# Eight-expert stage of a hybrid transformer: tokens gathered by indirect DMA from DRAM instead of by matmul, results parked in DRAM

## The chip, the cores and the metric

One NeuronCore of a Trainium2 chip runs the whole program. The metric is the device time of one execution in microseconds (us); the kernel before was timed in three runs, and one execution was profiled.

## The reference, cut to what matters

The program is two layers of a latent-diffusion trunk over 256 latent and 256 context tokens of width 1024, all in float32. The change touches the end of the second layer, where each of the 256 latent tokens goes to two of eight experts:

```python
def moe_swiglu(h, w_router, b_router, w_gate, w_up, w_down):
    logits = (h @ w_router + b_router).astype(jnp.float32)
    top_v, top_i = lax.top_k(logits, TOP_K)
    weights = jax.nn.softmax(top_v, axis=-1)
    combine = jnp.sum(jax.nn.one_hot(top_i, N_EXPERTS) * weights[..., None], axis=-2)
    y = jnp.zeros_like(h)
    for e in range(N_EXPERTS):
        y = y + combine[..., e:e + 1] * swiglu(h, w_gate[e], w_up[e], w_down[e])
    return y
```

Here h is the normalised and modulated token stream, `swiglu` is (silu(h Wg) * (h Wu)) Wd with 1024 -> 3584 -> 1024, and the result is scaled, added to the residual and normalised once more.

## The kernel before

**Precision.** Every large product is made of three fp32r matmuls (`mm3`, L212): high by high, high by low, low by high. So each weight tile of 128 x 2048 floats (a unit, 1 MB) is loaded from DRAM into a buffer `raw` by the SP queue (`load`, L156), copied to its rounded high part `wh` by ACT (L176), and its low part `wl` is subtracted by DVE (L177). There are three buffers of `wh` and `wl`, and eleven of `raw` in the expert stage.

**Experts.** For each expert up to 128 tokens are laid into 128 slots. The expert's hidden width is cut into seven chunks. A chunk takes two units of the gate weights, two of the up weights (`expert_in`, L1049, `half`, L1039), a transposition of the 128 x 512 result (`turn`, L1060: four PE transposes and a split into high and low), and two units of the down weights (`expert_out`, L1068), which is issued one chunk late. A unit is twelve matmuls of 512 columns, so a chunk is 72. Eight experts take 336 units.

**Tokens in.** `gather` (L1000) makes the slots' tokens by matmul: a 0/1 selection matrix `S` of 256 tokens by 128 slots (`slots`, L973) is multiplied with the tokens' high and low parts `hth`, `htl`, in eight groups of four matmuls of 128 columns, each group followed by one ACT and one DVE instruction which write `xg` (L1020, L1021). For experts 0 and 1 the tokens are not yet normalised, so that `S` carries the normaliser in two parts and a group has six matmuls. `normalize` (L986) then normalises `hth` and `htl` in place for the others.

**Results out.** When an expert's last chunk is done, its result stands in two PSUM tiles `ys`. `scatter_steps` (L1105) scales each, splits it into high and low, and multiplies it with the transposed `S` (`ST`, made by `slots_T`, L1080, with two PE transposes), two matmuls of 512 columns for each of two token tiles, and DVE adds the product, weighted by the token's share `cw`, to the residual `acc` (L1099). The last expert does this at once in plain float32 (`scatter_now`).

**Order.** `gather` and `normalize` are generators in a list `background`; `step` (L1031) advances the first by one yield behind every unit of gate or up weights. The framework then orders each engine's instructions itself: by program order, but one whose inputs it models as ready may be filled in ahead of an earlier one that it models as waiting. Weight loads are asked for eight units ahead, splits two units ahead.

Of the kernel before, what the change touches and what calls it, by code (L numbers as in the profile page):

```python
# [8 lines left out]
F32 = mybir.dt.float32  # L9
F32R = mybir.dt.float32r  # L10
# [6 lines left out]
P = 128  # L17
KD = 8
# [93 lines left out]
def _program(tc, A, out):  # L112
# [3 lines left out]
    def newpool(name, bufs, side="left"):  # L116
        return tc.alloc_tile_pool(name=name, bufs=bufs, side=side, reuse_waits="tile")
# [7 lines left out]
    pools = [const, rawp, whp, psp, smallp, xp]  # L125
# [13 lines left out]
    def ps_t():  # L139
        return psp.tile([P, 512], F32, tag="t", name=nm("pst"), bufs=2)  # L140
# [831 lines left out]

    def slots(p_, e, tag="S", by=None):  # L973
        if by is None:
            s_ = mop.tile([P, 2 * P], F32R, tag=tag, name=nm(tag), bufs=1)
        else:
            s_ = mop.tile([P, 512], F32R, tag=tag, name=nm(tag), bufs=1)[:, 0:2 * P]
        for tt in range(2):
            o, at = s_[:, tt * P:tt * P + P], p_[:, tt, e:e + 1]
            if by is None:  # L980
                vec.tensor_scalar(o, iota, at, None, ALU.is_equal)
            else:
                vec.tensor_scalar(o, iota, at, by[:, tt:tt + 1], ALU.is_equal, ALU.mult)
        return s_

    def normalize():  # L986
        for tt in range(2):
            for n in range(2):
                h, l = (t[:, tt, 512 * n:512 * n + 512] for t in (hth, htl))
                t, r = mop.tile([P, 512], F32, tag="yv", name=nm("t"), bufs=1), rs[:, tt:tt + 1]  # L990
                with tc.issue_after(first_gather[1].ins):
                    vec.tensor_scalar(t, l.bitcast(F32), r, None, ALU.mult)
                vec.scalar_tensor_tensor(t, h.bitcast(F32), r, t, ALU.mult, ALU.add)
                yield
                put_split(h, l, t)
                yield

    def gather(p_, e, raw=False):  # L1000
        S = []
        xg = mop1.tile([P, KD, 2, P], F32R, tag="xg", name=nm("xg"), bufs=2)

        def steps():
            if raw:
                s_ = slots(p_, e, "yh", rsh.bitcast(F32))
                terms = [(hth, s_), (htl, s_), (hth, slots(p_, e, "yl", rsl))]
            else:
                S.append(slots(p_, e))
                terms = [(hth, S[0]), (htl, S[0])]  # L1010
            yield
            for k in range(KD):
                pg = ps_mm() if front and k % 2 else ps_t()
                for i_, (hsrc, s_) in enumerate(terms):
                    for tt in range(2):
                        pe.matmul(pg[:, 0:P], lhsT=hsrc[:, tt, k * P:k * P + P], rhs=s_[:, tt * P:tt * P + P],
                                  start=(i_ == 0 and tt == 0), stop=(i_ == len(terms) - 1 and tt == 1))
                b = mod[:, 1, 24 + k, 0:1]
                hi, lo = xg[:, k, 0, :], xg[:, k, 1, :]
                ia = act.activation(hi, pg[:, 0:P], AF.Identity, bias=b)  # L1020
                iv = vec.scalar_tensor_tensor(lo, pg[:, 0:P], b, hi.bitcast(F32), ALU.add, ALU.subtract)  # L1021
                hold[:] = [ia, iv] if front else []
                yield
            if raw:
                S.append(slots(p_, e))
        return xg, S, steps()

    front = []
    background = []

    def step():  # L1031
# [3 lines left out]
    def drain(g):  # L1035
        for _ in g:
            pass
# [50 lines left out]
    def scaled(ys, n, tag="yv", bufs=1):  # L1088
        yv = mop.tile([P, 512], F32, tag=tag, name=nm(tag), bufs=bufs)
        vec.tensor_tensor(yv, ys[n], gf[:, 512 * n:512 * n + 512], ALU.mult)  # L1090
        return yv
# [10 lines left out]
        for n in range(2):  # L1102
            scatter(e, n, [(ST.bitcast(F32), scaled(ys, n, "a", 2))])

    def scatter_steps(e, ys, ST):  # L1105
        yv = scaled(ys, 0)
        for n in range(2):
            yh = mop.tile([P, 512], F32R, tag="yh", name=nm("yh"), bufs=1)
            yl = mop.tile([P, 512], F32R, tag="yl", name=nm("yl"), bufs=1)
            put_split(yh, yl, yv)  # L1110
            if n == 0:
                yv = scaled(ys, 1)
            yield
            scatter(e, n, [(ST, yh), (ST, yl)])

    prev = None
    xg, S, g = gather(pos, 0, True)
    front.append(0)
    drain(g)
    front.clear()  # L1120
    first_gather = list(hold)
    wp.release()
    xp.release()
# [12 lines left out]
    nxt, pend = (xg, S, g), []  # L1136

    def between():
        if prev is not None:
            turn(prev)  # L1140
        if pend:
            next(pend[0], None)

    def finish():
        expert_out(prev["e"], prev["c"], prev, prev["ys"])
        if prev["c"] == NCH - 1:
            pend[:] = [scatter_steps(prev["e"], prev["ys"], prev["ST"])]
            next(pend[0])
# [24 lines left out]
    between()  # L1173
    expert_out(prev["e"], prev["c"], prev, prev["ys"])
# [177 lines left out]
```

## Time and profile before

| | us |
|---|---|
| median of 3 runs (lowest to highest) | 1850.55 (1850.11 to 1851.01) |
| the profiled execution, its own time | 1851.12 |
| its span, first to last instruction | 1849.1 |

The expert stage fills the span from about 838 to 1837 us. Times in the rows further down are counted from the start of the span. PE is the matmul engine, PEld its weight loads, DVE the vector engine, ACT the scalar engine, POOL the GpSimd engine, SP the queue that issues the weight loads. A matmul's record lasts longer than its share of the engine, as successive matmuls overlap in the pipeline; the distance from start to start tells what one costs.

### The profile page before, as it was taken

Reading aid. Unit: us, or ns where it says so; the run is one execution under the profiler, and the core shown is the slowest. Engines: PE = TensorE matmul, PEld = TensorE weight load, DVE = VectorE, ACT = ScalarE, POOL = GpSimd, SP = SyncE. Lnnn points to the kernel's source line nnn. Section 1 sums busy time; section 2 is a strip of 40 time slices with the busy share of each in tenths; the row PEclk is TensorE's granted clock in tenths of the full one; section 3 lists DMA queues with packets and bytes.
Section 4 is the critical chain, followed back from the end, with each engine's and each line's share of the span. In section 5 each row is a group of like instructions: output and inputs, shape, how many; then the busy total and the mean of one; then the engine's idle time right before and its main releaser. Section 6 shows DMA issues by size and latency. Waiting matters only on the chain. (4 is left out here: it accounts for less than half of the span.)

```text
span 1849.1 us, 22123 instructions
## 1 busy us (share of the span) xinstructions
PE 1801.1 (97%) x8766; PEld 1438.1 (78%) x8766; DVE 1364.7 (74%) x1468; ACT 1039.8 (56%) x1082; POOL 0.2 (0%) x4
## 2 busy tenths in 40 slices
PE   6999998999999999999999999999999999999997
PEld 5775487888888878598888888888878888888885
DVE  5632645554455588658899899898898898988987
ACT  3323634222222245647677777777777777777774
POOL 0000000000000000000000000000000000000000
PEclk9999998999999999999999999999999999999999
DMA  9567321463344326039899999999999999999890
GB/s 364 186 234 267 122 96 57 151 225 137 114 160 168 114 54 199 22 137 358 329 354 370 326 370 356 348 350 362 352 339 356 351 351 352 367 351 347 331 416 35
DMA packets 68687, 475.03 MB, mean 257 GB/s; under 512 B 7520, under 2 KB 8160, under 8 KB 13024
## 3 DMA queue, kind: packets, MB, share of 16 engines
q1 hardware_dynamic: 66416, 469.27, 68.4%
q10 hardware_dynamic: 2160, 4.27, 0.7%
q8 instruction: 71, 1.16, 0.3%
q14 instruction: 40, 0.33, 0.1%
HBM read 470.36 MB, written 1.05 MB: 255 GB/s over the span
## 5 line engine op out<-in xcount | busy, mean ns | idle before, releaser
L177 DVE TENSOR_TENSOR wl<-raw,wh 128x2048 fp32r<-128x2048 f32 (+1 forms) x461 | 904.1, 1982 | 220.5 <-ACT wh L176 214.5
L176 ACT ACTIVATE wh<-raw 128x2048 fp32r<-128x2048 f32 (+1 forms) x461 | 763.3, 1670 | 415.9 <-PE mm L214 166.8
L213 PE MATMUL mm<-wh,xg 128*128 128x512 f32 x896 | 353.5, 395 | 0.0
L214 PE MATMUL mm<-wl,xg 128*128 128x512 f32 x896 | 352.3, 393 | 0.0
L215 PE MATMUL mm<-wh,xg 128*128 128x512 f32 x896 | 349.8, 390 | 0.0
L214 PEld LDWEIGHTS mm<-wl,xg 128*128 128x128 f32 x896 | 168.5, 188 | 35.1 <-DVE wl L177 1.8
L213 PE MATMUL mm<-hx,wh 128*128 128x512 f32 (+1 forms) x496 | 191.8, 391 | 3.8 <-ACT hx L400 3.8
L215 PEld LDWEIGHTS mm<-wh,xg 128*128 128x128 f32 x896 | 168.3, 188 | 34.2
L213 PEld LDWEIGHTS mm<-wh,xg 128*128 128x128 f32 x896 | 168.4, 188 | 33.6
L214 PE MATMUL mm<-hx,wh 128*128 128x512 f32 (+1 forms) x496 | 192.3, 388 | 0.0
L215 PE MATMUL mm<-hx,wl 128*128 128x512 f32 (+1 forms) x496 | 192.0, 387 | 0.0
L214 PE MATMUL pss<-wl,ahi 128*128 128x512 f32 x448 | 176.7, 395 | 1.3 <-DVE wl L177 1.3
L215 PE MATMUL pss<-wh,alo 128*128 128x512 f32 x448 | 174.4, 390 | 0.0
L213 PE MATMUL pss<-wh,ahi 128*128 128x512 f32 x448 | 168.2, 391 | 0.0
L213 PEld LDWEIGHTS mm<-hx,wh 128*128 128x128 f32 x496 | 94.3, 191 | 26.3 <-ACT hx L400 4.5
L214 PEld LDWEIGHTS mm<-hx,wh 128*128 128x128 f32 x496 | 94.4, 190 | 18.9
L215 PEld LDWEIGHTS mm<-hx,wl 128*128 128x128 f32 x496 | 94.1, 190 | 18.9
L214 PEld LDWEIGHTS pss<-wl,ahi 128*128 128x128 f32 x448 | 84.2, 188 | 20.3 <-DVE wl L177 3.9
L213 PEld LDWEIGHTS pss<-wh,ahi 128*128 128x128 f32 x448 | 84.2, 188 | 17.2
L215 PEld LDWEIGHTS pss<-wh,alo 128*128 128x128 f32 x448 | 84.2, 188 | 16.7
L409 DVE SCALAR_TENSOR_TENSOR x<-mm,mod,x 128x256 f32<-128x256 f32 x120 | 51.9, 478 | 38.8 <-PE mm L215 38.8
L215 PE MATMUL mm<-ah,wl 128*128 128x512 f32 x176 | 68.5, 389 | 0.0
(279 smaller groups left out, 1987.1 us busy)
## 6 DMA issues: line engine op xcount, KB each, us to landing
raw<-in_mg SPq DMA_DIRECT2D x112, 1024.0 KB, 7.1
raw<-in_mu SPq DMA_DIRECT2D x112, 1024.0 KB, 7.0
raw<-in_md SPq DMA_DIRECT2D x112, 1024.0 KB, 7.2
raw<-in_ada SPq DMA_DIRECT2D x48, 1024.0 KB, 5.3
raw<-in_na_in SPq DMA_DIRECT2D x10, 1024.0 KB, 5.8
raw<-in_fg SPq DMA_DIRECT2D x10, 1024.0 KB, 4.9
raw<-in_fu SPq DMA_DIRECT2D x10, 1024.0 KB, 4.9
raw<-in_fd SPq DMA_DIRECT2D x10, 1024.0 KB, 4.9
```

Of the source, the lines that this page charges most:

```text
L176: act.activation(h_, r_, AF.Copy)
L177: vec.tensor_tensor(l_, r_, h_.bitcast(F32), ALU.subtract)
L213: pe.matmul(ps, lhsT=lh, rhs=rh, start=start, stop=False)
L214: pe.matmul(ps, lhsT=lh, rhs=rl, start=False, stop=False)
L215: pe.matmul(ps, lhsT=ll, rhs=rh, start=False, stop=stop)
L409: vec.scalar_tensor_tensor(x[:, db, a:b], ps[:, a:b], mod[:, l, g0 + db, c:c + 1], x[:, db, a:b], ALU.mult, ALU.add)
```

## The change

A DRAM scratch `hrow` holds the 256 normalised tokens and `yrow` the results of seven experts. `normalize` now runs at the start of expert 0, adds the shift (transposed into rows, eight PE transposes), and stores four pieces of 256 KB to `hrow` through the POOL queue. `gather` for experts 1 to 7 computes the token number of each slot with two small matmuls of `S`, fetches 128 rows of 4 KB by an indirect DMA of the POOL queue into `xt`, and six yields later turns them with two groups of four PE transposes, each split by one ACT and one DVE instruction. For experts 0 to 6, `keep_rows` copies `ys` by ACT and stores two pieces of 256 KB to `yrow` through ACT's queue; there are no selection matmuls and no `ST` for them. At the start of expert 7, `fetch_rows` fetches each token's one or two rows by four indirect DMAs of 512 KB, and `combine` adds them, weighted, to `acc` in eight steps behind the units of the last two chunks. `row_numbers` computes the rows and weights with some twenty small DVE instructions. The first expert's gather is as it was. A gap tile grows from 56 to 72 words, which together with the new small tiles moves the fp32r operands behind it by a multiple of 256 bytes if each small tile takes a multiple of 32 bytes.

```diff
+    dramp = tc.alloc_tile_pool(name="dramp", bufs=1, space=bass.MemoryType.DRAM)
+    hrow = dramp.tile([TL, 1024], F32, tag="hrow", name="hrow")
+    yrow = dramp.tile([(NE - 1) * P, 1024], F32, tag="yrow", name="yrow")
...
-    mop.tile([P, 56], F32, tag="gap", name="gap2", bufs=1)
+    mop.tile([P, 72], F32, tag="gap", name="gap2", bufs=1)
...
     def normalize():
+        shift = []
+        for n in range(2):
+            pt = ps_t()
+            for j in range(4):
+                pe.transpose(pt[:, j * P:j * P + P], mod[:, 1, 24 + 4 * n + j, 0:1].to_broadcast([P, P]), ident)
+            shift.append(mop.tile([P, 512], F32, tag=("yh", "yl")[n], name=nm("shift"), bufs=1))
+            act.activation(shift[n], pt, AF.Copy)
+            yield
...
                 t, r = mop.tile([P, 512], F32, tag="yv", name=nm("t"), bufs=1), rs[:, tt:tt + 1]
                 with tc.issue_after(first_gather[1].ins):
-                    vec.tensor_scalar(t, l.bitcast(F32), r, None, ALU.mult)
+                    vec.scalar_tensor_tensor(t, l.bitcast(F32), r, shift[n], ALU.mult, ALU.add)
                 vec.scalar_tensor_tensor(t, h.bitcast(F32), r, t, ALU.mult, ALU.add)
+                nc.gpsimd.dma_start(hrow[tt * P:tt * P + P, 512 * n:512 * n + 512], t)
                 yield
-                put_split(h, l, t)
...
+    def gather(p_, e):
+        xg, S = new_xg(), []
+        def steps():
+            S.append(slots(p_, e))
+            yield
+            pi = ps_t()
+            for tt in range(2):
+                pe.matmul(pi[:, 0:2], lhsT=S[0][:, tt * P:tt * P + P].bitcast(F32), rhs=tokn[:, tt, :],
+                          start=(tt == 0), stop=(tt == 1))
+            idx = mop1.tile([P, 1], I32, tag="idx", name=nm("idx"), bufs=2)
+            vec.tensor_copy(idx, pi[:, 0:1])
+            xt = mop1.tile([P, 1024], F32, tag="htl", name=nm("xt"))
+            nc.gpsimd.indirect_dma_start(xt[:, :], None, hrow[:, :], bass.IndirectOffsetOnAxis(ap=idx[:, 0:1], axis=0))
+            for _ in range(6):
                 yield
+            for h in range(2):
+                pg = ps_t()
+                for j in range(4):
+                    pe.transpose(pg[:, j * P:j * P + P], xt[:, (4 * h + j) * P:(4 * h + j) * P + P], ident)
+                hi, lo = xg[:, 4 * h:4 * h + 4, 0, :], xg[:, 4 * h:4 * h + 4, 1, :]
+                put_split(hi, lo, pg.rearrange("p (k s) -> p k s", s=P))
                 yield
...
-    def scatter_steps(e, ys, ST):
+    def keep_rows(e, ys):
         for n in range(2):
+            yv = mop.tile([P, 512], F32, tag=("yh", "yl")[n], name=nm("yv"), bufs=1)
+            act.activation(yv, ys[n], AF.Copy)
+            nc.scalar.dma_start(yrow[e * P:e * P + P, 512 * n:512 * n + 512], yv)
...
+    def fetch_rows():
+        for tt in range(2):
+            yy = mop1.tile([P, 2, 1024], F32, tag=("hth", "xg")[tt], name=nm("yy"), bufs=1 + tt)
+            fetched.append(yy)
+            for i_ in range(2):
+                ri = mop1.tile([P, 1], I32, tag="nj", name=nm("nj"), bufs=4)
+                vec.tensor_copy(ri, rows[i_][0][:, tt:tt + 1])
+                nc.gpsimd.indirect_dma_start(yy[:, i_, :], None, yrow[:, :],
+                                             bass.IndirectOffsetOnAxis(ap=ri[:, 0:1], axis=0))
+    def combine():
+        for tt in range(2):
+            yy = fetched[tt]
+            for n in range(2):
+                h_ = slice(512 * n, 512 * n + 512)
+                a, b = yy[:, 0, h_], yy[:, 1, h_]
+                vec.tensor_scalar(a, a, rows[0][1][:, tt:tt + 1], None, ALU.mult)
+                vec.scalar_tensor_tensor(a, b, rows[1][1][:, tt:tt + 1], a, ALU.mult, ALU.add)
+                yield
+                vec.tensor_tensor(a, a, gf[:, h_], ALU.mult)
+                vec.tensor_tensor(acc[:, tt, h_], acc[:, tt, h_], a, ALU.add)
+                yield
...
             if c == 2:
-                ST = slots_T(S[0])
                 if e < NE - 1:
-                    nxt = gather(pos, e + 1, e == 0)
+                    nxt = gather(pos, e + 1)
                     background.append(nxt[2])
-                if e == 0:
-                    background.append(normalize())
+                else:
+                    ST = slots_T(S[0])
+                if e == 1:
+                    background.append(row_numbers())
+            if e == NE - 1 and c == 0:
+                fetch_rows()
+            if e == NE - 1 and c == 4:
+                background.append(combine())
```

## Rows read from the trace of the kernel before

**Rows 1.** The page's first part: busy time of each engine, its share of the span and its instructions.

```profile
PE 1801.1 (97%) x8766; PEld 1438.1 (78%) x8766; DVE 1364.7 (74%) x1468; ACT 1039.8 (56%) x1082; POOL 0.2 (0%) x4
```

**Rows 2.** Busy time by stretch: the expert stage, the part of it in which weights are loaded, and 40 us at the end of the loading. Columns: stretch, its length, then each engine's busy time and instructions, the granted PE clock, the DMA engines' busy share, GB/s.

```profile
838.00:1837.00 999.00, 992.75 (x4585) 818.03 (x4583) 886.52 (x599) 724.72 (x537) 0.00 (x0) 1.00 0.91 343
838.00:1806.00 968.00, 962.15 (x4455) 794.34 (x4454) 860.44 (x580) 707.38 (x521) 0.00 (x0) 1.00 0.94 354
1760.00:1800.00 40.00, 40.00 (x182) 33.09 (x181) 35.42 (x20) 29.48 (x20) 0.00 (x0) 1.00 1.01 419
```

**Rows 3.** Groups of instructions by line in the expert stage (838 to 1837 us): line, engine, operation, tiles, shapes, count, then busy time and mean ns of one, and the idle time before them.

```profile
L177 DVE TENSOR_TENSOR wl<-raw,wh 128x2048 fp32r<-128x2048 f32 x335 | 759.0, 2282 | 86.0 <-ACT wh L176 80.2 <-DMA raw<-in_md 3.7 <-DMA raw<-in_mg 1.1
L176 ACT ACTIVATE wh<-raw 128x2048 fp32r<-128x2048 f32 x335 | 639.8, 1913 | 165.0 <-PE mm L215 88.3 <-PE pss L215 64.2 <-DMA raw<-in_md 5.6
...
L1099 DVE SCALAR_TENSOR_TENSOR acc<-mm,cw,acc 128x512 f32<-128x512 f32 x32 | 23.2, 745 | 8.3 <-PE mm L1097 7.8
...
L1016 PE MATMUL pst<-S,hth 128*128 128x128 f32 x96 | 17.0, 248 | 1.0 <-DVE xg L1021 1.0
...
L1097 PE MATMUL mm<-yh,ST 128*128 128x512 f32 x28 | 11.2, 418 | 0.0
...
L218 ACT ACTIVATE yh<-yv 128x512 fp32r<-128x512 f32 x14 | 8.8, 626 | 1.4 <-DVE yv L1090 1.3
...
L1083 PE MATMUL pst<-c_ident,S 128*128 128x128 f32 x16 | 3.0, 271 | 0.0
L993 DVE SCALAR_TENSOR_TENSOR t<-hth,rs_y,t 128x512 f32<-128x512 f32 x4 | 3.0, 751 | 0.1
...
L1016 PE MATMUL pst<-yh,hth 128*128 128x128 f32 x16 | 2.9, 261 | 0.8 <-DVE xg L1021 0.8
...
L992 DVE TENSOR_SCALAR t<-htl,rs_y 128x512 f32<-128x512 f32 x4 | 1.9, 480 | 0.0
```

**Rows 4.** The round of one unit, in order of time (start, duration, engine, line, operation): PE ends a unit, ACT splits the unit three further on, DVE subtracts its low part (the row covers two units in a row), and PE first uses that low part. Between the two PE rows stand two whole units, with nothing but these matmuls: 26 steps from start to start.

```profile
1341.44 0.39 PE L215 MATMUL mm<-wh,xg 128*128 128x512 f32 x1
...
1341.87 1.92 ACT L176 ACTIVATE wh<-raw 128x2048 fp32r<-128x2048 f32 x1 [0.30 <-PE mm L215]
...
1341.60 4.52 DVE L177 TENSOR_TENSOR wl<-raw,wh 128x2048 fp32r<-128x2048 f32 x2 [0.80 <-ACT wh L176]
...
1347.34 0.39 PE L214 MATMUL pss<-wl,ahi 128*128 128x512 f32 x1
```

**Rows 5.** PE in order of time around one gather group of four matmuls (L1016): the matmul ahead of it, the group's first two, and the second matmul behind it.

```profile
1301.47 0.39 PE L215 MATMUL mm<-wh,xg 128*128 128x512 f32 x1
1301.70 0.33 PE L1016 MATMUL pst<-S,hth 128*128 128x128 f32 x2
...
1302.38 0.40 PE L214 MATMUL mm<-wl,xg 128*128 128x512 f32 x1
```

**Rows 6.** The same around a gather group of six (expert 1): the matmul ahead of it and the second one behind it.

```profile
896.92 0.39 PE L215 MATMUL mm<-wh,xg 128*128 128x512 f32 x1
...
898.04 0.40 PE L214 MATMUL pss<-wl,ahi 128*128 128x512 f32 x1
```

**Rows 7.** The same around a pair of scatter matmuls (L1097): the matmul ahead of it and the first one behind it.

```profile
1477.82 0.39 PE L213 MATMUL mm<-wh,xg 128*128 128x512 f32 x1
...
1478.50 0.39 PE L214 MATMUL mm<-wl,xg 128*128 128x512 f32 x1
```

**Rows 8.** The same around the two transposes of `ST` (L1083): the matmul ahead of them and the second one behind them.

```profile
1260.18 0.39 PE L215 MATMUL pss<-wh,alo 128*128 128x512 f32 x1
...
1260.86 0.39 PE L214 MATMUL mm<-wl,xg 128*128 128x512 f32 x1
```

**Rows 9.** The same around the four transposes of `turn` (L1063): the matmul ahead of them and the second one behind them.

```profile
1304.65 0.39 PE L215 MATMUL mm<-wh,xg 128*128 128x512 f32 x1
...
1305.55 0.40 PE L214 MATMUL mm<-wl,xg 128*128 128x512 f32 x1
```

**Rows 10.** Every wait of PE in the expert stage: who waited for whom, us in total, times, longest us.

```profile
PE pst L1063 <- DVE xg L1021: 2.8, 4, 0.7
PE pst L1016 <- DVE xg L1021: 1.8, 5, 0.6
PE pss L214 <- DVE wl L177: 1.3, 4, 0.7
```

**Rows 11.** The waits of SP's queue in the expert stage, in the same columns.

```profile
SPq L161 <- DVE wl L177: 647.0, 258, 8.5
...
SPq L161 <- DMA fg<-in_fg_row: 10.1, 2, 9.9
```

**Rows 12.** The last two weight loads as SP issues them, and the last unit as ACT splits it (in two halves).

```profile
1796.64 2.53 SPq L161 DMA_DIRECT2D raw<-in_md  x2
...
1825.96 2.00 ACT L176 ACTIVATE wh<-raw 128x1024 fp32r<-128x1024 f32 x2
```

**Rows 13.** DMA issues: target and source, queue, count, KB each, median us from issue to landing; and one issue of 256 KB as ACT's queue makes it.

```profile
raw<-in_mg SPq DMA_DIRECT2D x112, 1024.0 KB, 7.1
...
mkT<-krot SPq DMA_DIRECT2D x1, 2048.0 KB, 14.7
...
fg<-in_fg_row ACTq DMA_DIRECT2D x2, 256.0 KB, 2.9
...
1749.26 0.33 ACTq L1164 DMA_DIRECT2D fg<-in_fg_row  x1
```

More of the change, by code (lines that the diff above doesn't have):

```diff
@@ new lines, in new_xg, with first_gather_steps @@
+    def new_xg():
+        return mop1.tile([P, KD, 2, P], F32R, tag="xg", name=nm("xg"), bufs=2)
+    def first_gather_steps(xg):
+        s_ = slots(pos, 0, "yh", rsh.bitcast(F32))
+        terms = [(hth, s_), (htl, s_), (hth, slots(pos, 0, "yl", rsl))]
+        for k in range(KD):
+            pg = ps_mm() if k % 2 else ps_t()
+            for i_, (hsrc, s_) in enumerate(terms):
+                for tt in range(2):
+                    pe.matmul(pg[:, 0:P], lhsT=hsrc[:, tt, k * P:k * P + P], rhs=s_[:, tt * P:tt * P + P],
+                              start=(i_ == 0 and tt == 0), stop=(i_ == len(terms) - 1 and tt == 1))
+            b = mod[:, 1, 24 + k, 0:1]
+            hi, lo = xg[:, k, 0, :], xg[:, k, 1, :]
+            ia = act.activation(hi, pg[:, 0:P], AF.Identity, bias=b)
+            iv = vec.scalar_tensor_tensor(lo, pg[:, 0:P], b, hi.bitcast(F32), ALU.add, ALU.subtract)
+            hold[:] = [ia, iv]
@@ new lines, in row_numbers @@
+    def row_numbers():
+        sm = lambda t, w=8: mop1.tile([P, 2, w] if w > 1 else [P, 2], F32, tag=t, name=nm(t))
+        last = NE - 1
+        val, wv, eq = sm("nv"), sm("nw"), sm("ne")
+        vec.tensor_scalar(wv, pos, float(P) + 0.5, None, ALU.is_lt)
+        vec.tensor_tensor(wv, wv, msk, ALU.mult)
+        vec.memset(wv[:, :, last:last + 1], 0.0)
+        vec.tensor_tensor(val, pos, base.unsqueeze(1).to_broadcast([P, 2, 8]), ALU.add)
+        vec.tensor_tensor(val, val, wv, ALU.mult)
+        vec.tensor_tensor(wv, wv, cw, ALU.mult)
+        yield
+        for i_ in range(2):
+            row = sm(f"nr{i_}", 1)
+            vec.tensor_reduce(row, val, AX.X, ALU.max)
+            vec.tensor_tensor(eq, val, row.unsqueeze(2).to_broadcast([P, 2, 8]), ALU.is_equal)
+            t = sm("nt")
+            vec.tensor_tensor(t, eq, wv, ALU.mult)
+            w = sm(f"nc{i_}", 1)
+            vec.tensor_reduce(w, t, AX.X, ALU.add)
+            if i_ == 0:
+                vec.tensor_tensor(wv, wv, t, ALU.subtract)
+                vec.tensor_tensor(eq, eq, val, ALU.mult)
+                vec.tensor_tensor(val, val, eq, ALU.subtract)
+            vec.tensor_scalar(row, row, -1.0, 0.0, ALU.add, ALU.max)
+            ri = mop1.tile([P, 2], I32, tag=f"ni{i_}", name=nm("ni"))
+            vec.tensor_copy(ri, row)
+            rows.append((ri, w))
+            yield
@@ new lines, in _program @@
+    rows = []
+    def fetch_rows():
+        for tt in range(2):
+            yy = mop1.tile([P, 2, 1024], F32, tag=("hth", "xg")[tt], name=nm("yy"), bufs=1 + tt)
+            fetched.append(yy)
+            for i_ in range(2):
+                ri = mop1.tile([P, 1], I32, tag="nj", name=nm("nj"), bufs=4)
+                vec.tensor_copy(ri, rows[i_][0][:, tt:tt + 1])
+                nc.gpsimd.indirect_dma_start(yy[:, i_, :], None, yrow[:, :],
+                                             bass.IndirectOffsetOnAxis(ap=ri[:, 0:1], axis=0))
@@ new lines, in _program @@
+    fetched = []
+    def combine():
+        for tt in range(2):
+            yy = fetched[tt]
[7 more added lines that the diff above has]
+                vec.tensor_tensor(acc[:, tt, h_], acc[:, tt, h_], a, ALU.add)
+                yield
@@ L1116, in _program @@
     prev = None
[L1117 to L1120, printed above, removed]
+    xg = new_xg()
+    first_gather_steps(xg)
     first_gather = list(hold)
@@ L1135, in _program @@
     vec.tensor_tensor(cw, cw, ws.unsqueeze(2).to_broadcast([P, 2, 8]), ALU.mult)
-    nxt, pend = (xg, S, g), []
+    nxt = (xg, [], iter(()))
+    tokn = mop1.tile([P, 2, 2], F32, tag="tokn", name="tokn")
+    row0 = mop.tile([P, P], F32, tag="S", name="row0", bufs=1)
+    vec.tensor_tensor(row0, ident, iota, ALU.mult)
+    vec.tensor_reduce(tokn[:, 0, 0:1], row0, AX.X, ALU.add)
+    vec.tensor_scalar(tokn[:, 1, :], tokn[:, 0, 0:1].to_broadcast([P, 2]), float(P - 1), None, ALU.add)
+    vec.tensor_scalar(tokn[:, 0, :], tokn[:, 1, :], -float(P), None, ALU.add)
+    base = mop1.tile([P, 8], F32, tag="base", name="base")
+    vec.tensor_scalar(base, iota[:, 0:8], -1.0, float(P), ALU.add, ALU.mult)
+    background.append(normalize())
     def between():
@@ L1140, in between @@
             turn(prev)
-        if pend:
-            next(pend[0], None)
     def finish():
@@ L1146, in finish @@
         if prev["c"] == NCH - 1:
-            pend[:] = [scatter_steps(prev["e"], prev["ys"], prev["ST"])]
-            next(pend[0])
+            keep_rows(prev["e"], prev["ys"])
     ST = fg = None
```

34 lines of the change are left out of this document (1 added, 33 removed).

## The prediction, made before the changed kernel was run

> **What bounds the kernel now.** I read the page's busy shares first, then the expert stage by stretch, then PE's rows in order of time, and last who waits for whom. PE is busy 97% of the span [rows 1] and 992.8 of 999.0 us in the expert stage [rows 2]. A busy PE need not be a full one, so the distance from start to start decides: from 1341.44 to 1347.34 us there are 26 steps in 5.90 us, 0.227 us each [rows 4]. The stage has 336 units of 12 matmuls, 4032 x 0.227 = 915 us. Of 999 us, 84 are something else on PE: transposes, gather, scatter, and waits. That is the ground on which this change works, if nothing else is close to being the bound.
>
> Two things are close. First the round of a unit [rows 4]: PE ends unit j-3 (last start 1341.44 plus 0.39), ACT splits unit j until 1343.79, DVE has the low part at 1346.12, PE needs it at 1347.34. So 1.2 us are spare, and ACT or DVE work put into a round in one piece beyond 1.2 us stalls PE. Second the transport: 354 GB/s while weights are loaded, the DMA engines 94% busy [rows 2]. But SP waits 647 us for DVE to free a `raw` buffer [rows 11], so a load is issued when there is room, not when the DMA is free; the last loads are issued at 1796.6 to 1799.2 us and the last split begins at 1825.96, some 27 us later, where landing takes 7.1 [rows 12, 13]; and for 40 us the same transport ran at 419 GB/s [rows 2]. PE is the bound.
>
> **What leaves PE.** An insertion's cost is the distance around it less the ordinary steps in it.
> - Gather of experts 2 to 7: 96 `S,hth` rows at two a group are 48 groups [rows 3]. 1301.47 to 1302.38 is 0.91, less two steps 0.454: 0.456 us [rows 5]. 48 x 0.456 = 21.9.
> - Gather of expert 1: 16 / 2 = 8 groups of six [rows 3], 898.04 - 896.92 - 0.454 = 0.67 [rows 6]: 5.3.
> - Scatter of seven experts: 28 pairs [rows 3], 0.68 - 0.227 = 0.453 [rows 7]: 12.7.
> - `ST` of seven experts, 7 of the 8 pairs in L1083's 16 [rows 3], 0.68 - 0.454 = 0.226 [rows 8]: 1.6.
> - PE's waits, all at gather, scatter or just behind: 5.9 us in 13 [rows 10]. A wait is counted from the end of the record before, 0.39 long, while the next would have started after 0.227, so 13 x 0.163 = 2.1 more: 8.0.
>
> Together 49.5 us.
>
> **What comes onto PE.** A group of four transposes costs 0.90 - 0.454 = 0.446 [rows 9]. Seven gathers with two groups each: 6.2. Their two index matmuls: no such row; below the `ST` pair's 0.226 there is no row of two instructions, above it stands a gather group's 0.456 [rows 5]; I take 0.226 (same stationary width, hardly any columns), 1.6. `normalize`'s eight transposes: 0.9. Together 8.7, so PE's own work falls by 40.8 us.
>
> **What may make PE wait.** These are bounded, not read.
> - `normalize` has one buffer `t`; each of its three later pieces waits until the store has read it, and DVE waits with it, the next `wl` behind. A piece is two instructions of 0.75 [rows 3]; a store of 256 KB is nearest to the load of that size, 2.9 us under full load, at most a whole weight load's 7.1 [rows 13]. Within three units of 2.72: 3 x (1.5 + 2.9 - 2.72) - 1.2 = 3.8, or with 7.1 16. Below, nothing: the order on DVE is filled by readiness, and the same buffer cost DVE 0.1 us before [rows 3]. I take 3.
> - `keep_rows` puts two ACT copies of about 0.63 and two issues of 0.33 [rows 3, 13] between splits: 1.9 where `yh` and `ST` took 1.6 spread wider. 0 to 7 x (1.9 - 1.2) = 5; I take 2.
> - `combine` is sixteen DVE instructions on 512 columns, 4 x (0.48 + 3 x 0.75) = 10.9 us by the rows of that width [rows 3]. DVE idles 999.0 - 886.5 = 112 us in the stage, 14 per expert [rows 2], which holds it: 0. Kept at its written places, the four gate and up units of a chunk ask DVE for 4 x 2.28, half of `combine` (5.5) and the chunk's own two instructions of that width (1.5), 16.1, where PE takes 4 x 2.72 + 0.45 = 11.3. The deficit of 4.8 meets the spare 1.2 in the first chunk and the 2 x (2.72 - 2.28) = 0.9 that the down units give back in the second: 3.6 + 3.9 = 7.5. I take 2.
> - The small instructions of `row_numbers` and the new constants need only what the router leaves; they fall into DVE's gaps: 0 to 2, I take 1. The new gather's first steps may wait as the old one's did, 0.36 + 0.16 each: 0 to 3.6, I take 1.
> - The gathered rows: from the fetch to the first transposes lie six yields, 96 matmuls with the down weights between, 21.8 us, and a turn: 22.2. POOL issues nothing in this trace; 512 KB lie between 2.9 for 256 KB and 14.7 for 2 MB [rows 13]. All are covered: 0. `yrow` needs longer (four fetches, at worst 59 us) and has four chunks of 72 steps and a turn, 67 us.
> - The transport: 10.5 MB more (1 stored and 3.7 gathered of `hrow`, 3.7 stored and 2.1 fetched of `yrow`). From 838 to 1806 us 968 x 354 = 343 MB came [rows 2]; in a stage 32 us shorter that asks for 353.5 MB in 936 us, 378 GB/s, against the 419 seen: 0.
>
> Together 9 us, between 0 and 34.
>
> The row of the transport shows 419 GB/s for 40 us, at a PE clock as before [rows 2]. The Trainium skill ("DMA: Bandwidth & Descriptors", "Where 436 GB/s comes from") says that loads from HBM are bound at about 358 GB/s per core. By the row the sum stands; by that rule the added bytes and the shorter stage could not be had and the time would come out near rival 3's. The trace does not agree with the rule over those 40 us.
>
> **The sum.** The profiled execution took 1851.1 us; 1851.1 - 40.8 + 9 = 1819.3. The median of the runs is 0.6 below that execution: 1819 us. By the bounds of the waits, 1810 to 1844; its own range is 1809 to 1835.
>
> **Rivals.**
> 1. *Fetched rows come late.* PE stands at the transposes with everything behind it queued. If a fetch, with the index and the descriptors made on POOL, takes X us, each of seven experts loses X - 22.2. At 26 us that gives 1819 + 7 x 3.8 = 1846; with X = 24 to 28, 1832 to 1860. Against it stands a cover over twice any row of that size.
> 2. *POOL holds DVE* (slower). Writing and reading descriptors for 4 stores, 7 gathers and 4 fetches, POOL may lock DVE out for h us each, and `wl` is late by it. PE loses 15 x (h - 1.2). Above h = 3.3 this eats the whole 31 us; at 4 us it gives 1819 + 42 = 1861. Only the small spare of 1.2 us speaks for it; no row shows POOL at work beside DVE. The Trainium skill ("SBUF — State Buffer", "Who interferes with whom") says that a DVE instruction with two SBUF inputs, as L177 is, and a GpSimd instruction that reads SBUF block each other, the later one for the whole of the earlier; by it a fetch may start one `wl` late, or a `wl` one fetch late. No run here shows it yet.
> 3. *The transport is the bound* (no gain, or slower). Were 354 GB/s the ceiling, 353.5 MB would take 999 us and loading end at 1837; the last split 27 us after a load is then down to 7 of landing, so the tail behind the loads, 1849.1 - 1799.2 = 50, is 30, and the time 1867. It decides below 378. SP's waits and the 419 GB/s speak against it. For it: SP once stood 9.9 us behind a DMA that ACT issued [rows 11], and the change has ACT issue 14. If each of seven pairs costs SP that, the rest must run at 353.5 / (936 - 69) = 408 GB/s, just under the 419.
> 4. *The offset of the fp32r operands matters and is not kept.* What a step then costs no row shows; if 0.227 became 0.234 on all 4032, it is 28 us and the gain is gone: 1847. Against it: the sizes add up to a whole multiple of 256 bytes if they are rounded to 32.
>
> **How the numbers follow.** Forecast 0.70 (1809 to 1835); the same with the waits at their upper ends 0.08 (1835 to 1844); late rows 0.08; POOL on DVE 0.05; transport 0.05; offset 0.04. Above 1844 lie most of the last four, about 0.17, and 0.03 lie below 1808 if still more of PE's odd steps go. So the range is 1808 to 1844. A measurement of this kernel tells about 0.2%, 3.7 us, from no change. Slower: 0.04 of POOL, 0.03 of transport and 0.01 of late rows, 0.08; same, 0.04: half of the offset's and a little of each other rival; faster, the rest, 0.88.
>
> **What would show it.** In the changed profile: no L1097 in experts 0 to 6; PE's start-to-start still 0.227; the stage some 32 us shorter, an expert near 967 / 8 = 121 us in place of 125; PE's waits near 9 us, most of them in expert 0's first two chunks (behind `t`) and in expert 7; loading near 375 GB/s with SP still waiting for DVE. Wrong would be: PE waits at the transposes of `xt` (rival 1), `wl` longer than 2.28 us while POOL works (2), ACT's or DVE's splits waiting for `raw` (3), steps above 0.227 (4).

## The result, and the profile of the changed kernel

The changed kernel took 1840.4 us (median; 1839.0 to 1840.6) against 1850.8 before: ratio 0.9942, 95% interval 0.9926 to 0.9957. The forecast was 1819. The time lies inside the range (1808 to 1844), but only 10.4 us of the expected 31.5 came. The comparison is of fast runs; a fourth run of the kernel before, of 6385 us, is not one of them. Below, the expert stage counts from the first start of its matmuls to the last: 994.0 us before, 983.0 in the changed kernel.

Busy time by stretch, columns as in [rows 2]: the stage, the part of it in which weights are loaded, four microseconds of expert 0 (the third figure from the end is the granted PE clock), and the begin of expert 7 in slices of 5 us.

```profile
838.00:1827.00 989.00, 968.75 (x4369) 792.74 (x4368) 854.30 (x516) 712.19 (x488) 17.98 (x15) 0.99 0.90 357
838.00:1796.00 958.00, 938.94 (x4242) 769.71 (x4242) 828.22 (x496) 694.85 (x470) 17.98 (x15) 0.99 0.93 368
866.00:870.00 4.00, 4.00 (x12) 3.09 (x12) 4.00 (x5) 0.43 (x1) 0.14 (x1) 0.57 0.80 284
1695.00:1700.00 5.00, 5.00 (x26) 4.14 (x25) 4.00 (x3) 2.29 (x4) 0.00 (x0) 1.00 0.09 35
1700.00:1705.00 5.00, 3.69 (x17) 2.74 (x16) 3.35 (x2) 3.45 (x3) 0.00 (x0) 1.00 0.66 193
1705.00:1710.00 5.00, 4.08 (x18) 2.85 (x16) 1.23 (x1) 0.00 (x0) 0.00 (x0) 1.00 1.00 406
1710.00:1715.00 5.00, 0.82 (x2) 0.45 (x3) 2.29 (x1) 4.55 (x4) 3.53 (x3) 0.77 1.01 412
1715.00:1720.00 5.00, 4.98 (x12) 3.55 (x12) 0.01 (x1) 1.66 (x2) 1.44 (x2) 0.55 1.01 415
1720.00:1725.00 5.00, 2.27 (x6) 1.77 (x7) 4.77 (x5) 1.69 (x1) 0.00 (x0) 0.80 1.02 420
```

Where [rows 2] had PE idle for 6 of 999 us, it now idles for 20 of 989, although less is asked of it. In the first 30 us of expert 7 the transport first starves (35 GB/s), then runs at its best rate, PE does 12 instructions in a slice that holds 22 at full speed, and the granted clock falls to 0.55.

The waits of PE and of SP in the stage (838 to 1827), as in [rows 10, 11], and DVE's wait for the fetched rows. (`mm` are the gate and up products, `pss` the down products.)

```profile
PE mm L217 <- DVE wl L180: 10.8, 10, 1.8
PE pss L217 <- DVE wl L180: 4.9, 2, 2.8
PE mm L216 <- ACT wh L179: 3.3, 1, 3.3
...
SPq L164 <- DVE wl L180: 682.8, 278, 8.7
SPq L164 <- DMA yrow<-yv: 119.2, 14, 15.5
SPq L164 <- DMA fg<-in_fg_row: 10.5, 2, 5.3
...
DVE yy L1184 <- DMA yy<-yrow,nj: 5.3, 1, 5.3
```

PE's waits for `xg` in [rows 10] are gone; in their place it waits, 19 us in 13 pieces, for splits. SP stood behind the fourteen stores of `yrow` for 119 us. To see where it costs time, the stage's 336 units are cut into eight runs of 42, an expert's number, in the order in which PE does them. Each run counts from its first matmul to the next run's first, the last one to the first matmul of the stage's last unit; every run but the first begins two units into its expert (us, experts 0 to 7):

| kernel | e0 | e1 | e2 | e3 | e4 | e5 | e6 | e7 |
|---|---|---|---|---|---|---|---|---|
| before | 125.5 | 124.9 | 124.8 | 124.8 | 124.9 | 124.4 | 124.4 | 117.8 |
| changed | 124.4 | 119.2 | 121.1 | 121.0 | 121.3 | 121.0 | 120.7 | 131.8 |

Experts 1 to 6 gained 3.4 to 5.7 us each, expert 0 1.1, and expert 7 lost 14.

**A boundary between two experts** (1 to 2), in order of time: `keep_rows`' first copy and its issue, the split that they hold up, `wl` behind it, the second copy and issue, and PE.

```profile
1091.86 0.60 ACT L221 ACTIVATE ahi<-pst 128x512 fp32r<-128x512 f32 x1 [1.69 <-PE pst L1087]
1093.02 0.60 ACT L1132 ACTIVATE yv<-pss 128x512 f32<-128x512 f32 x1 [0.56 <-PE pss L218]
1093.65 0.33 ACTq L1133 DMA_DIRECT2D yrow<-yv  x1
1094.08 1.92 ACT L179 ACTIVATE wh<-raw 128x2048 fp32r<-128x2048 f32 x1 [0.46 <-DVE alo L222]
1095.90 0.58 ACT L1132 ACTIVATE yv<-pss 128x512 f32<-128x512 f32 x1
1096.02 2.29 DVE L180 TENSOR_TENSOR wl<-raw,wh 128x2048 fp32r<-128x2048 f32 x1 [2.08 <-ACT wh L179]
1096.50 0.33 ACTq L1133 DMA_DIRECT2D yrow<-yv  x1
1098.37 0.50 PE L217 MATMUL mm<-wl,xg 128*128 128x512 f32 x1 [1.28 <-DVE wl L180]
```

ACT is free at 1092.46, but the copy stands ahead of the split in its order and has to wait for PE's last matmul of that half; with the issue the split starts 1.62 us late, more than the spare 1.2 us. PE loses 1.45 us here, and 1.47 to 1.74 at each of the five boundaries that follow.

**The begin of expert 7**: SP's issues, then ACT, DVE, POOL and PE in order of time.

```profile
1684.88 16.24 SPq L164 DMA_DIRECT2D raw<-in_mg  x2
1701.22 6.06 SPq L164 DMA_DIRECT2D raw<-in_mu  x2
...
1698.71 0.33 ACTq L1133 DMA_DIRECT2D yrow<-yv  x1
...
1701.57 0.33 ACTq L1133 DMA_DIRECT2D yrow<-yv  x1
...
1710.45 1.91 ACT L179 ACTIVATE wh<-raw 128x2048 fp32r<-128x2048 f32 x1 [6.55 <-DMA raw<-in_mu]
1710.86 0.94 POOL L1173 DMA_INDIRECT yy<-yrow,nj  x1 [110.11 <-DMA yrow<-yv]
1712.41 0.56 PE L216 MATMUL mm<-wh,xg 128*128 128x512 f32 x1 [3.34 <-ACT wh L179]
1714.74 0.80 PE L217 MATMUL mm<-wl,xg 128*128 128x512 f32 x1 [1.76 <-DVE wl L180]
...
1719.99 0.48 DVE L1184 TENSOR_SCALAR yy<-yy,nc 128x512 f32<-128x512 f32 x1 [5.31 <-DMA yy<-yrow,nj]
1722.73 0.63 PE L217 MATMUL pss<-wl,ahi 128*128 128x512 f32 x1 [2.76 <-DVE wl L180]
```

Here two chains meet. In the compiled order the DMAs of SP and of ACT take eight completion counters in turn, so a load that comes after a store on the same counter waits until that store has landed. At every boundary two loads wait so (18.2 us around 1090); here the two `fg` loads, which ACT also issues, come between them as well and four loads wait, 28.7 us in all: the second `mg` for 15.5 us, and `raw` is late for ACT by 6.55. Most of the 15.5 us is not the store's own time: it is issued only at 1698.71, as its copy waits for PE, and has landed at 1700.7. Then all that was held back goes out at once: the last store takes 8.4 us to land, the fetch can't start before, and DVE has `combine`'s first multiply in its order well ahead of the chunk where it is written, with a `wl` behind it. PE stands for 3.3, 1.8 and 2.8 us, and from the second of these stalls on its clock is granted at half for most of the time (0.77, 0.55 and 0.80 in the three slices from 1710 on; half is the level of 1.2 GHz): between 1715.3 and 1726.2 17 steps are 0.427 us long and not 0.227, which with the steps at either end is another 4 us.

### The profile page after: what moved, and what is told of

Its sections match the earlier page's. It is cut to its first block, busy times and chain, and to the rows that moved or that the text cites. A ratio compares the mean times of both kernels' runs of the same rounds, so it can differ in the third digit from the quotient of the medians.

```text
span 1838.4 us, 21638 instructions
## 1 busy us (share of the span) xinstructions
PE 1776.8 (97%) x8548; PEld 1412.0 (77%) x8548; DVE 1334.4 (73%) x1413; ACT 1026.9 (56%) x1031; POOL 18.2 (1%) x19
## 5 line engine op out<-in xcount | busy, mean ns | idle before, releaser
L216 PE MATMUL pss<-wh,ahi 128*128 128x512 f32 x448 | 162.1, 393 | 0.0
L218 PEld LDWEIGHTS pss<-wh,alo 128*128 128x128 f32 x448 | 85.0, 190 | 16.6
L221 ACT ACTIVATE ahi<-pst 128x512 fp32r<-128x512 f32 x56 | 33.5, 598 | 72.6 <-PE pst L1087 72.6
```

What stands on the lines that cost most here:

```text
L216: pe.matmul(ps, lhsT=lh, rhs=rh, start=start, stop=False)
L218: pe.matmul(ps, lhsT=ll, rhs=rh, start=False, stop=stop)
L221: return (act.activation(hi, src, AF.Copy), vec.tensor_tensor(lo, src, hi.bitcast(F32), ALU.subtract))
```

## The experiments

The theory (A): the gather and the sum over PE's work are as forecast, and what is lost lies in three places, expert 7 (the stores in one planned order with SP's loads), the boundaries (the copies and issues on ACT) and expert 0 (one buffer `t`). The rival (B): the fetch itself eats it, by its bytes and by DVE's wait for it.

**pool_store**

```
-            nc.scalar.dma_start(yrow[...], yv)
+            nc.gpsimd.dma_start(yrow[...], yv)
```

> The only edit: the two stores that keep an expert's result are issued by GpSimd's queue and not by ScalarE's. Theory A (the last expert's loss comes from the stores standing in one planned order with SP's loads): SP's waits for these stores, 119.2 us in the changed kernel with 15.5 us the longest, go to nothing; the last expert, 131.8 us, falls to 121 to 125; and as ScalarE no longer issues two DMAs (0.33 us and some 0.4 us of gap each) in a round, the PE wait of 1.47 us at each of six boundaries falls to about 0.7. In all 10 to 14 us faster than the changed kernel: about 1828 us, 0.988 of the kernel before. Theory B (it comes from the fetch: its four transfers, and VectorE standing at the combination's first instruction): SP's waits go, but the last expert stays at 129 or more and the time at 1835 to 1838.

Measured 1830.9 us, 0.9898 (0.9882 to 0.9913). Expert 7 took 127.9, experts 2 to 6 120.0 to 120.3 where it had been 120.7 to 121.3, and PE's loss at a boundary fell from 1.45 to 0.90. The waits of SP in its stage, and DVE's from 1680 us on:

```profile
SPq L164 <- DVE wl L180: 786.8, 316, 8.6
SPq L164 <- DMA fg<-in_fg_row: 20.6, 2, 11.5
...
DVE yy L1184 <- DMA yy<-yrow,nj: 5.1, 1, 5.1
```

The waits for the stores are gone and 9.5 us with them: 3.9 in expert 7, 3.9 in experts 2 to 6, and 1.3 in expert 0, which the edit doesn't touch. (Expert 0 lies between 122.2 and 124.4 in the profiles of all kernels here that leave its one buffer and its steps as they are; why is open. A gain of 1 or 2 us counts below only where it shows in its place.) So the stores cost time. But expert 7 stayed between the two theories: DVE's wait for the fetched rows remained, PE stood 6.1 us behind it (the longest of its waits in this profile), and the `fg` loads now hold SP twice as long. A and B each own a part of expert 7.

**late_fetch**

```
-            if e == NE - 1 and c == 0:
+            if e == NE - 1 and c == 3:
                 fetch_rows()
...
-            if e == NE - 1 and c == 4:
+            if e == NE - 1 and c == 5:
                 background.append(combine())
```

> The only edit: the parked rows are fetched after the fourth of the last expert's eight chunks instead of after the first, and the combination starts two chunks after that instead of four after the other; the stores stay where they were. Theory A (stores in SP's planned order): SP's 15.5 us wait at the last boundary stays, and with it the first two PE stalls (3.7 and 2.3 us) and a part of the halved clock; only the third stall (3.15 us, VectorE behind the fetched rows) goes: 3 to 5 us, about 1836 us. Theory B (the fetch): all of them go, the last expert falls from 131.8 to about 121 us and the time to 1828 to 1830.

Measured 1837.2 us, 0.9926 (0.9911 to 0.9941); expert 7 130.5. The time is near A's, but the kernel tests neither theory. An expert has seven chunks, not eight as written there, and so only four of the combination's eight steps fit: the second 128 tokens' parked rows are not added, and eight VectorE instructions are missing from this time. And the compiled order did not follow the written one: the first fetch and the first multiply stand where they stood.

```profile
1708.79 0.93 POOL L1173 DMA_INDIRECT yy<-yrow,nj  x1 [110.25 <-DMA yrow<-yv]
1717.89 0.49 DVE L1184 TENSOR_SCALAR yy<-yy,nc 128x512 f32<-128x512 f32 x1 [5.28 <-DMA yy<-yrow,nj]
```

That is 23 us after the first matmul of expert 7's run, as in the changed kernel (1710.86), and the third stall of PE, which should have gone by A and by B, is there at its full 2.8 us. Of the gain of 3.2 us, 2.2 lie in expert 0, which the edit doesn't touch, and 1.3 in expert 7, from which the eight instructions are missing. What it gives to hold the multiply back in the compiled order is shown by hold_combine.

**two_t**

```
-                t = mop.tile([P, 512], F32, tag="yv", ..., bufs=1)
+                t = mop.tile([P, 512], F32, tag="yv", ..., bufs=2)
```

> The only edit: the normalized rows of the first expert's stage go through two buffers in turn instead of one. If the single buffer is what holds VectorE (1.72 us waiting for the store before) and costs PE 2.6 us and a stretch of halved clock: the first expert falls from 124.4 to about 121.5 us and the time to about 1837.5 us. If it is the place of these eight VectorE instructions in front of the splits: no change of the first expert, 1840, or worse where the planner now puts four in a row.

Measured 1836.6 us, 0.9925 (0.9911 to 0.9938); expert 0 went from 124.4 to 121.4. PE's wait there, 2.17 us behind a DVE that had stood 1.72 us for the store, is 0.8 with two, and the clock, halved at 866 to 870 us before, stays up: both were the single buffer's.

**gather_alone**

```
-            keep_rows(prev["e"], prev["ys"])
+            pend[:] = [scatter_steps(prev["e"], prev["ys"], prev["ST"])]
+            next(pend[0])
...
-                fetch_rows()
-                background.append(combine())
```

> One part alone: the tokens come from DRAM as in the changed kernel, but each expert's result is added to the sums by the old scatter of matmuls, with its transposed slots. By the terms of the prediction the gather removes 27.2 us of PE, adds 8.7 and costs 4 us of waits: about 14.5 us faster than before, 1836. If the sizes seen in the changed kernel hold (four index matmuls and not two, 4.5 to 5 us for the normalizing), about 1838. Theory A, that the loss lies in the parked results: the last expert takes 117 to 119 us, as before, with no SP wait for stores. If instead the gather's side is what ate the gain, this kernel is no faster than 1846.

Measured 1840.1 us, 0.9938 (0.9923 to 0.9953), and expert 7 119.0: no loss at the end, but less gain elsewhere than the terms give. Its profile has something that no kernel above shows. The first and the last matmul of one down-projection unit, 11 steps apart, with no wait between:

```profile
1058.20 0.39 PE L215 MATMUL pss<-wh,ahi 128*128 128x512 f32 x1
...
1060.77 0.39 PE L217 MATMUL pss<-wh,alo 128*128 128x512 f32 x1
```

That is 2.57 us (0.2335 a step) where the changed kernel takes 2.49. Leaving out the parked rows' small tiles had moved the tiles behind them, among them the turned products `ahi` and `alo`, which are the stationary operand of these matmuls.

**gather_kept**

```
-    mop.tile([P, 72], F32, tag="gap", ...)
+    mop.tile([P, 96], F32, tag="gap", ...)
```

> gather_alone once more, with the gap tile at 96 floats instead of 72. In gather_alone the median step of the down-projection's matmuls was 0.231 to 0.237 us where every other kernel has 0.227; with the small tiles of the parked rows left out, the turned products lay 64 bytes past a multiple of 256 bytes in their partition, and the weights 160. The wider gap puts them at 160 again. Theory O (the offset sets the step): the steps are back at 0.227, about 7 us come off, 1833; then the gather's side gave 18 us and the parked rows cost about 7.5 net. Rival (the slower steps belong to the scatter's traffic): the steps stay and the time stays at 1840.

Measured 1831.5 us, 0.9895 (0.9880 to 0.9910), 8.5 us under gather_alone. The same unit:

```profile
1054.79 0.39 PE L215 MATMUL pss<-wh,ahi 128*128 128x512 f32 x1
...
1057.28 0.39 PE L217 MATMUL pss<-wh,alo 128*128 128x512 f32 x1
```

2.49 us again; 0.076 us in each of 112 units is 8.5 us, the whole difference. So gather_alone had a second edit in it without my meaning one, and the clean division is this: **the gather from DRAM gives 19.5 us by itself, and the parked rows, as they were made, take 9 of them back.**

**gap56** (the changed kernel with the gap at 56)

> The changed kernel with the gap tile back at 56 floats, nothing else. Theory O: the turned products lie 96 bytes past a multiple of 256, the weights 160; the down-projection's 1344 steps take 0.231 to 0.237 us and the time is about 7 us over the changed kernel's 1840.4: 1847. Rival (the gap is no part of the time): 1840.

Measured 1842.4 us, 0.9955 (0.9940 to 0.9971): some 2 us over the changed kernel, not 7, and the two intervals overlap. The trace is clearer: a unit's 11 steps took 2.52 us in the median, which makes 3 us in 112 units. The offset sets the step, but by how much depends on the offset: 64 bytes 0.076 us a unit, 96 bytes 0.028.

**The ladder.** Each of the next five carries the edits of those above it, with the stores on GpSimd's queue as the first rung.

**hold_combine**

```
+                with tc.issue_after(begin.ins):     # begin: product of expert 7's chunk c == 4
                     vec.tensor_scalar(a, a, rows[0][1][...], None, ALU.mult)
```

> On top of the stores from GpSimd's queue (1830.9 us): the combination's multiplies of the fetched rows may not issue before the product of the last expert's fourth chunk has. In the kernel with only the stores moved, VectorE still stood 5.05 us at the first of them and PE 6.1 us behind it, and the clock halved after that. Theory A1 (that wait is what is left of the last expert's loss): the last expert falls from 127.9 to 118 to 120 us and the time to about 1822. Theory A2 (SP's 20.6 us behind the two fg rows that ScalarE loads is late next): PE then waits for weights at the same boundary, the last expert stays at 123 or more, 1826 or above.

Measured 1828.3 us, 0.9876 (0.9859 to 0.9892); expert 7 123.9. (The chunk is the fifth; the text counts wrongly.) The stall of 6.1 us and the halved clock behind it went. Expert 7 is only 4 us shorter, because the combination now stands in one lump at its end, where PE waits for it (priced by the last two kernels). SP still waits:

```profile
SPq L164 <- DMA fg<-in_fg_row: 21.0, 2, 11.6
```

and PE lost 1.3 us at two more places in the begin of expert 7, behind late splits, as A2 says.

**fg_pool**

```
-                    nc.scalar.dma_start(fg[n], ...)
+                    nc.gpsimd.dma_start(fg[n], ...)
```

> On top of hold_combine: the two fg rows of the last expert are loaded by GpSimd's queue. Theory A1: SP's waits for them (20.6 us in two) go, but the raw buffers covered them: within 1 us of hold_combine. Theory A2: PE's wait for late weights goes with them: 3 to 6 us faster than hold_combine, about 1822.

Measured 1826.0 us, 0.9864 (0.9848 to 0.9880); expert 7 122.3. The late splits in the begin of expert 7 are gone, as A2 says; expert 7 is 1.6 us shorter, less than A2 expected, and expert 0, which the edit doesn't touch, 1.2.

**ladder_t** (two_t on top)

> On top of fg_pool: two buffers in turn for the normalized rows. The effects are in different experts, so the 3.8 us that it gave by itself should come off again: 3 to 4 us faster than fg_pool, about 1818. If stalls only move on to the next wait, less than 1.5.

Measured 1823.8 us, 0.9852 (0.9836 to 0.9869): 2.2 us, between the two. Expert 0 had 123.0 us in fg_pool's profile and has 121.3 here; with the single buffer it lay between 122.2 and 124.4, so the changed kernel's 124.4 was a dear case: its clock was halved there for 3.4 us, and in fg_pool it was not.

**ladder_keep**

```
     def keep_rows(e, ys):
...
+            with tc.issue_after(last_wh[0].ins):
                 act.activation(yv, ys[n], AF.Copy)
             nc.gpsimd.dma_start(yrow[...], yv)
+            yield
...
-            keep_rows(prev["e"], prev["ys"])
+            background.insert(0, keep_rows(prev["e"], prev["ys"]))
```

> On top of ladder_t: the two ScalarE copies that take an expert's result out of PSUM become steps of the next expert's second chunk, each behind a split, and the fetch is called one chunk later. Where ScalarE's copy in front of a split is what makes PE wait at the six boundaries (0.9 us each with the stores moved): about 5 us faster than ladder_t, 1813. If the wait comes from the turn of the boundary itself (the transposes, VectorE's subtraction and the split between them), which this edit leaves: within 1 us of ladder_t.

Measured 1817.9 us, 0.9821 (0.9805 to 0.9838): 5.9 us. Experts 2 to 5 went from 120.3 to 119.3, and no PE wait is left at the boundaries. The turn was not the cause; the copy ahead of the split was.

**ladder_spread**

```
-                    vec.tensor_scalar(a, a, rows[0][1][...], None, ALU.mult)
+                with tc.issue_after(last_wh[0].ins):
+                    act.activation(a, a, AF.Identity, scale=rows[0][1][...])
                 yield
+                with tc.issue_after(last_wl[0].ins):    # as for each of the three on VectorE
                     vec.scalar_tensor_tensor(a, b, rows[1][1][...], a, ALU.mult, ALU.add)
...
-            if e == NE - 1 and c == 4:
+            if e == NE - 1 and c == 2:
```

> On top of ladder_keep (1817.9 us): the combination is spread over the last expert's chunks four to seven, one VectorE instruction behind each of twelve splits, and the multiply by the first weight goes to ScalarE. In ladder_keep VectorE did sixteen of them in the last chunks and PE waited eight times, 0.35 to 0.75 us over a step each, 4 us in all. If those waits are VectorE's lack of room: 2 to 4 us faster, 1814 to 1816. If they come with the end of the loads: no change.

Measured 1811.2 us, 0.9786 (0.9773 to 0.9800): 6.7 us, more than expected; expert 7 115.2. (The hold of hold_combine is dropped in it; the places behind the splits take its part.) The stage while weights are loaded, 40 us in it, and all of PE's waits in the stage:

```profile
838.00:1764.00 926.00, 925.11 (x4225) 764.41 (x4225) 821.24 (x483) 693.29 (x472) 28.59 (x31) 1.00 0.98 380
1700.00:1740.00 40.00, 40.00 (x185) 33.01 (x184) 36.99 (x24) 30.63 (x23) 9.25 (x5) 1.00 1.02 419
```

```profile
PE pss L218 <- DVE wl L180: 0.7, 1, 0.7
PE mm L218 <- DVE wl L180: 0.2, 1, 0.2
```

PE is busy for 925.1 of 926.0 us. This is the fastest of the kernels here that compute the whole result, 29 us under the changed kernel.

**no_combine**

> ladder_keep without the combination: the parked rows are fetched and never added, so seven experts' results are left out of the output and the sixteen VectorE instructions out of the time. What it gains over ladder_keep is the price of the combination there: 4 to 5 us by PE's waits (1813), against 2 in the forecast's sum; under 1 us if those waits have another cause.

Measured 1811.4 us, 0.9782 (0.9767 to 0.9797), 6.5 us under ladder_keep: the price of the combination in one lump. Spread, it costs nothing that shows: ladder_spread has it and is as fast. Nor do the fetched bytes by themselves, the other half of theory B: both of these kernels fetch them, and neither waits for them.

## Why the prediction was right in its sum and wrong in its time

**What PE does: right.** The 994.0 us of the stage before are 915.0 of steps (4031 of 0.227) and 79.0 of all else, its waits among it, as the forecast's 49.5 had 8.0 of them. In the changed kernel the distances over everything that is not an expert's matmul, less the ordinary steps in them, add up to 36.2: 42.8 less (40.8 forecast). The transposes of `xt` cost 0.448 a group (0.446 forecast). The index matmuls run as four instructions a gather and cost 0.46, not 0.226, 1.6 us more in all; so 10.4 us came and not 8.7, and what left was about 53 us and not 49.5. That the difference came out so near is in part luck: the two misses point opposite ways.

```profile
L1047 PE MATMUL pst<-c_ident,xt 128*128 128x128 f32 x56 | 8.4, 271 | 0.0
L1036 PE MATMUL pst<-tokn,S 128*128 128x2 f32 x28 | 3.5, 230 | 0.0
```

The step stayed 0.227. Without the 9 us of waits the forecast's sum is 1810; ladder_spread, with nearly no waits, took 1811.2.

**What PE waits for: wrong.** This is the step that failed: the forecast took 9 us of waits out of 0 to 34, because it bounded them by durations and mean rates, at the places where the instructions are written. The 983.0 us of the changed kernel's stage are 915.0 of steps, 36.2 of the other work and 31.8 of stalls, slow steps among them; ladder_spread has 3.7 of these. That the time lies inside the range all the same is luck: its upper end holds 16 us for `normalize`'s stores, which cost 3, while `keep_rows` went beyond its bound and the stores' order and the clock had no term. The difference of 28 to 29 us is made up by place (expert by expert against ladder_spread): 3.0 in expert 0, 9.1 in experts 1 to 6, 16.6 in expert 7. Term by term, expert 7 by the ladder's order, which another order would divide otherwise:

- *`keep_rows`*: 2 taken, 5 the bound, 9 measured (1.45 to 1.74 at each of six boundaries; ladder_keep and pool_store took them off). What failed is "7 x (1.9 - 1.2)": it added durations. The first copy needs PE's last matmul of its half, so the split behind it in ACT's order waits for PE as well; its delay is counted from when ACT was free (1092.46) to 1094.08.
- *Fetch of `yrow`* and *`combine`*: 0 and 2 taken. The cover of 67 us was counted from the place where `combine` is written. The order of the engines is not the written one: its first multiply stood in DVE's order three to four chunks earlier, where the rows had just been asked for, and a `wl` behind it. Held back from there (hold_combine) it gave 4.0 us of expert 7; then it met the other mechanism, DVE's lack of room, which the forecast bounded at 7.5 and which measured 6.5 (no_combine). `combine`'s place and its lump cost 4.0 + 6.0 of expert 7's 16.6 us (the steps of hold_combine and ladder_spread); the stores account for 3.9, `fg` for 1.6 and the copies for 1.1.
- *The transport and SP*: 0 taken. Rival 3 named the cause, SP 9.9 us behind a DMA that ACT issued, but it put 9.9 us to each of seven pairs, 69 in all, where 119.2 came, 17 a pair; and it was priced only as a rate that the rest must keep. At six boundaries SP stood 7.5 to 19.0 us and ACT waited for no `raw` that cost PE time. At the seventh the `fg` loads stood in the same order, SP stood 28.7 us, and the slack of the buffers ran out. Beyond that slack a queue that stands is a stall for those behind it, whatever the mean rate is.
- *`normalize`*: 3 taken, 3.0 in expert 0 (3.8 by the times) measured, by the mechanism described.
- *The clock* had no term. PE had stood 3.3 us and was standing again, for 1.8, when the grant fell; it was 0.55 for the slice of 5 us from 1715 on, and the steps at 1.2 GHz cost about 4 us of expert 7 beyond the waits themselves.

**The rivals.** 1: PE never waited at the transposes of `xt`; the gathered rows land in 9.0 us (below), against a cover of 22.2. 2: not seen as a cost: the 14 `wl` that ran beside an instruction of POOL took 2.289 us on average, the other 319 took 2.290 (2.282 before). But a block shows the other way round. A fetch that starts just ahead of a `wl` keeps POOL for 0.94 us; one that starts within a `wl` is held until 0.8 us after that `wl`'s end (in the second pair below the first of the two `wl` in the row ends at 1599.94, the fetch at 1600.76):

```profile
1113.71 0.94 POOL L1041 DMA_INDIRECT xt<-hrow,idx  x1 [97.23 <-DVE idx L1039]
1113.75 4.49 DVE L180 TENSOR_TENSOR wl<-raw,wh 128x2048 fp32r<-128x2048 f32 x2
...
1597.65 4.50 DVE L180 TENSOR_TENSOR wl<-raw,wh 128x2048 fp32r<-128x2048 f32 x2
1598.00 2.76 POOL L1041 DMA_INDIRECT xt<-hrow,idx  x1 [120.06 <-DVE idx L1039]
```

By the Trainium skill's rule cited in the prediction ("SBUF — State Buffer", "Who interferes with whom") such an instruction of DVE and one of GpSimd that reads SBUF block each other, the later one waiting. The trace agrees as far as the fetch is the later one; a `wl` held back by a fetch is not seen. 3: as a ceiling, no: 368 GB/s in the changed kernel's loading, 380 over 926 us of ladder_spread and 419 for 40 us. The Trainium skill has another page for this ("Perfetto Trace Analysis", "Roofline"): the 358 GB/s are a core's share when both cores of a pair read, and one that runs alone can go up to what its 16 DMA engines give, about 435. The trace agrees, with up to 420 GB/s in the slices of 5 us above. 4: the offset was kept (160 bytes, before and after), and it matters: see gather_kept.

DMA issues of the changed kernel, columns as in [rows 13]:

```profile
yrow<-yv ACTq DMA_DIRECT2D x14, 256.0 KB, 7.9
...
hrow<-t POOLq DMA_DIRECT2D x4, 256.0 KB, 5.3
...
xt<-hrow,idx POOLq DMA_INDIRECT x7, 9.0
yy<-yrow,nj POOLq DMA_INDIRECT x4, 12.0
```

`normalize`'s stores of 256 KB land in 5.3 us, where the forecast used 2.9 from a load of that size, "at most a whole weight load's 7.1"; those of `yrow` take 7.9.

## What to carry to other kernels

A sum of what leaves and comes onto the bounding engine holds well; what spoils it is order. For each new instruction ask where the compiled order may put it, what stands behind it there and what it waits for: a copy that waits for PE ahead of a split, a multiply that waits for a fetch ahead of a `wl`, a store that a load's counter waits for. And when a part is taken out to be measured alone, see that the tiles which stay keep their addresses.

## What was not expected of the hardware

- The address of an fp32r operand, taken modulo 256 bytes, changes the pace of matmuls that wait for nothing. By the addresses in the compiled programs, with the moving operand (the expert's weights `wh`, `wl`) at 160: 11 steps take 2.49 us with the stationary one (the turned products) at 160 as well, 2.52 at 96, 2.57 at 64. Whether it is the address by itself or the distance to the other operand, and why, is open; other offsets were not tried.
- Three stalls close together, 3.3, 1.8 and 2.8 us, cost half as much again by the clock, about 4 us: its grant fell to 0.55 in a slice of 5 us, and the steps that followed the second and the third stall took 0.427 us until 1726.2.
- DMAs from GpSimd's queue cost the other engines nothing that shows here: with 14 more of them (pool_store) experts 2 to 6 are faster than with the same stores on ACT. An indirect one is itself held up by a `wl` in progress: 2.76 us on POOL where it otherwise takes 0.94. A store from there is not (0.54 us within a `wl`).
